# Turning a normalised activation on VectorE in 32x32 blocks, in one layer of a hybrid encoder

## The chip, the core and the metric

The kernel runs on one core of a Trainium2 chip. Its time is the device time of one execution in microseconds. The names of the engines in the profile are PE (TensorE's matmuls), PEld (TensorE's weight loads), DVE (VectorE), ACT (ScalarE), POOL (GpSimd) and SP (SyncE, which here only issues DMAs). Two runs are compared by their medians; a single profiled execution gives the trace.

## The reference

One encoder layer on 2048 tokens of 1024 features, all float32:

```python
h  = rms_norm(x, norm_mix)
z  = h @ w_in                       # 1024 x 4352, split into q, k, v of two attentions and two gates
yA = windowed_gqa(qA, kA, vA, sink) # 8 heads of 64, window 128
yB = neighborhood_attn(qB, kB, vB, rpb)   # 32 x 64 grid, 8 x 16 neighbours
gates  = sigmoid(gate + b_gate)
merged = gateA * (yA @ w_proj_a) + gateB * (yB @ w_proj_b)
x  = x + merged @ w_out
h2 = rms_norm(x, norm_mlp)
x  = x + square(relu(h2 @ w_up)) @ w_down
out = rms_norm(x, norm_final)
```

rms_norm divides each token's row by its root mean square and multiplies each feature by a gain.

## The kernel before

Tokens go in four blocks of 512 (BT). A float32 product is made from three TensorE passes: each operand is split into a rounded high part, a cast on ScalarE, and the rest, a subtraction on VectorE or GpSimd (`split`, L246 to L249), and `mm3s` issues high x high, high x low and low x high (L252 to L254; `mm3` with L201 to L203 likewise). The large projections use a seven-product scheme over quarters (`in_quad`, `up_quad`), whose sums and differences of quarters are made on VectorE and GpSimd.

TensorE contracts over the partitions, so an activation must stand with features on partitions. After normalisation it stands with tokens on partitions, and has to be turned. Before the change TensorE does this against an identity matrix, in tiles of 128x128, and ScalarE evicts the result from PSUM with the feature's gain as the scale, which by then is one number per partition.

The stages, in the order of the profile:

- The in-projection of blocks 0 and 1 (to about 335 us). Both blocks are turned in SBUF (`turned`, `scaled`, `scaled_less`), and seven pages of h, the right operands of the seven products, are built from them. The page for product 5 is the first whose sum runs on GpSimd (the loop over `halves(t1)` after `normalised(xp, tiles[1], by_scalar=True)`). The square roots of a normalisation are also GpSimd operations (`rstd_of`, L229), so on that engine they stand in one row with these sums. While quads q = 5 and 6 run, blocks 2 and 3 of x are normalised, turned by 64 TensorE transposes (L242), evicted into two buffers `ze` (L464) and stored to DRAM in `h1d` (L602).
- Attention A (about 335 to 700) with the in-projection of blocks 2 and 3, whose pages `h_pages` loads from `h1d` and splits; then attention B (to about 1010).
- Four blocks b of gates, merge and out-projection (about 1010 to 1437). `gated` projects y and multiplies by the gate; POOL adds the two branches, `mh` and `ml` (L1265, L1266) are the split sum, the out-projection adds to x (`xr`, L1284), and the result is normalised, turned by 32 TensorE transposes for each block (L1295), evicted with `g_mlp` (L1301) and stored to `h2d` from the ScalarE queue (L174). In block 3 the evictions go into the space of `mh`.
- The up projection (about 1437 to 2077). `up_right` loads blocks of `h2d` and builds the pages `ubh1` to `ubh7` of the seven products; the one for product 2 is loaded into `urb`. `up_quad` takes the products in the order 1, 5, 6, 2, 7, 4, 3 and stores the squared activations. `up_start` prepares the first pages and weights ahead of the last block's out-projection.
- The down projection (about 2077 to 2680), with the final normalisation.

A scheduler orders the instructions of each engine from the program and its pools of buffers; `tc.issue_after(x)` forces an instruction behind another. Each engine works through its own row in order and waits at its head, and so does each DMA queue's issuer (SP, and the ScalarE queue).

Of the kernel before, what the change touches and what calls it, by code (L numbers as in the profile page):

```python
# [22 lines left out]
P = 128  # L23
# [69 lines left out]
def encoder_layer(ctx, tc, x, norm_mix, w_in, b_gate, sink, rpb, w_pa, w_pb, w_out,  # L93
# [39 lines left out]
    g_mlp = cp.tile([P, KC], F32, name="g_mlp")  # L133
# [80 lines left out]
    def load_tile(pl, tag, bufs, rows):  # L214
        t = T(pl, [P, D], F32, tag, bufs)
        last_dma[0] = SY.dma_start(t, rows).ins
        return t

    def rstd_of(pl, t, jp=None, mean=False):

        st = T(pl, [P, 4], F32, "st", 4)
        junk = T(pl if jp is None else jp, [P, 512], F32, "junk", 1)
        for n in range(2):
            A.activation(junk, t[:, n * 512 : (n + 1) * 512], AF.Square, scale=float(D) ** -0.5 if mean else 1.0,
                         accum_out=st[:, n : n + 1])
        r = st[:, 2 : 3]
        V.scalar_tensor_tensor(out=r, in0=st[:, 0:1], scalar=EPS if mean else D * EPS, in1=st[:, 1:2],
                               op0=ALU.add, op1=ALU.add)
        G.tensor_tensor(out=r, in0=r, in1=power, op=ALU.pow)  # L229
        return r  # L230

    def normalised(pl, tiles, jp=None, by_scalar=False):

        for t in tiles:
            if by_scalar:
                A.activation(t, t, AF.Copy, scale=rstd_of(pl, t, jp, True))
            else:
                V.tensor_scalar(t, t, rstd_of(pl, t, jp), float(D) ** 0.5, ALU.mult, ALU.mult)

    def turned(ps, tiles, k):  # L240
        for t in range(4):
# [240 lines left out]
    tiles[1] = x_tiles(xp, 1, 8)  # L482
    ws1.append(row_half(*QUADS[1], 1))
    with tc.issue_after(last_dma[0]), nc.allow_non_contiguous_dma(reason="small per-feature vectors"):
        SY.dma_start(g_mlp, norm_mlp[0].rearrange("(k p) -> p k", p=P))
# [15 lines left out]
    next(quad0)  # L501
    next(quad0)
    normalised(xp, tiles[1], by_scalar=True)
    for o, h, l in zip(halves(t1), *map(halves, right[1])):
        add(G, o, h.bitcast(F32), l.bitcast(F32))
    next(quad1)
    next(quad1)

# [72 lines left out]
    for q in range(2, len(QUADS)):  # L581
        if q == 5:
            s_v.close()
            in_v2.pop()
            xp = pools(s_z, "right", ("xin", "st"), "x2")
        if q == 7:
            bias_tables()
        lf = list(in_left(ws, 256, (1, 2) if q == 2 else ()))
        if q + 1 < len(QUADS):
            ws = in_weights(*QUADS[q + 1])  # L590
        if q in (5, 6):

            b = q - 3
            xt = x_tiles(xp, b, 3)
            normalised(xp, xt, Junk())
            for k in range(0, KC, 2):
                ht = in_e()
# [4 lines left out]
                SY.dma_start(h1d[b - 2][k * P : (k + 2) * P, :].rearrange("(k p) t -> p k t", p=P), ht)  # L602
# [338 lines left out]
    flush(queue=SY)  # L941
    s_b.close()
    s_pg = ExitStack()
    p4 = pools(s_pg, "right", ("page", "yraw", "z"), "m")

    def load_y(b):
        yh, yl = [], []
# [27 lines left out]
    p4x = pools(s_wo, "left", ("xr", "junk", "mh", "ml"), "m")  # L975

    p4x["st"] = cp
    wo = []

    def load_wo(n):  # L980
# [169 lines left out]
        parts(3, b22)  # L1150

    def squared(c, src=None):
        A.activation(c, c if src is None else src, AF.Relu)  # L1153
        A.activation(c, c, AF.Square)

    def up_quad(m, q, lf, right, spread):

        x, y, z = [None] * 2, [None] * 2, [None] * 2
        c1, u2, c11, c22 = [None] * 2, [None] * 2, [None] * 2, [None] * 2

        def keep(n, a, c):
            stored[0] = SY.dma_start(ats[n][2 * q + a][:, m], c).ins

        for n in (1, 5, 6, 2, 7, 4, 3):
            hl, (rh, rl) = lf[n], right[n]
            last = None
            for a in range(2):
# [9 lines left out]
                    mm3s(ps, hl[:, 0, k, at], hl[:, 1, k, at], rh[:, k], rl[:, k], k == 0 and n in (1, 5, 6), k == 3)  # L1177
                if n == 1:
                    c1[a] = up_rings["c"]()
                    A.copy(c1[a], ps)  # L1180
                elif n == 6:
                    u2[a] = up_rings["c"]()
                    last = add(V, u2[a], ps, c1[a])
                elif n == 2:
                    c11[a] = up_rings["c"]()
                    squared(c11[a], ps)
                    keep(1, a, c11[a])
                elif n == 7:
                    c22[a] = up_rings["c"]()
                    add(V, c22[a], ps, c1[a])  # L1190
                    last = add(V, c22[a], z[a], c22[a])
                    squared(c22[a])
                    keep(4, a, c22[a])
                elif n == 4:
                    last = add(V, c1[a], ps, c1[a])
                    squared(c1[a])
                    keep(2, a, c1[a])
                elif n == 3:
                    a11, a12, a21, a22 = c11[a], c1[a], u2[a], c22[a]
                    last = add(V, a21, ps, a21)  # L1200
# [27 lines left out]
    for b in range(NB):  # L1228
# [59 lines left out]
        flush()  # L1288
        if b < NB - 1:
            next_y = load_y(b + 1)  # L1290
        normalised(p4x, tiles)
        for k in range(KC):
            ps = psum("av", 1) if b < NB - 1 or k % 3 == 0 else psum("pt", 2)
            for t in range(4):
                PE.transpose(ps[:, t * P : (t + 1) * P], tiles[t][:, k * P : (k + 1) * P], ident)  # L1295
# [5 lines left out]
            A.activation(ht, ps, AF.Copy, scale=g_mlp[:, k : k + 1])  # L1301
# [215 lines left out]
```

## Time and profile before

| | |
|---|---|
| runs | 2684.27, 2681.82, 2678.03 us; median 2681.82 |
| profiled execution | 2680.99 us, its span 2679.2 us |
| mean granted TensorE clock | 0.998 |
| PE busy | 2613.9 us, 98% of the span |
| DVE / ACT / POOL busy | 1535.4 (57%) / 1260.7 (47%) / 839.1 (31%) |
| DMA | 490.28 MB moved, mean 183 GB/s |

A row of the profile's groups names line, engine, operation, written and read buffers, count, busy time and mean duration in ns, and then the time that its engine sat idle ahead of it, with what released it. A row of the timeline gives start, duration, engine, operation, and in brackets the idle time before it and its releaser. A row of a source line's view gives the shortest, median and longest duration in ns and the first and last start. A row of the waits gives waiting and releasing operation, total us, times, longest.

### The profile page before, as it was taken

The page shows a single profiled execution, that of the slowest core. Times are in us where ns is not written, and L with a number is a line of the kernel's source. Part 1 is how long each engine was busy: PE and PEld are TensorE (multiplying, and loading weights), DVE is VectorE, ACT ScalarE, POOL GpSimd, SP SyncE. Part 2 cuts the span into 40 slices and gives each one's busy share as a digit, 9 for nine tenths or more (in the row PEclk, how much of TensorE's full clock was granted, in tenths as well). Part 3 has the DMA queues.
Part 4 walks back from the last instruction along what each step waited for, and adds up shares of the span by engine and source line. Part 5 has one row for each costly group of instructions (what it writes and reads, how often), then busy time and mean ns, then how long its engine had stood idle before and what let it go on. Part 6 is the DMA issues. An engine that isn't in the chain of part 4 may idle for free. (4 is left out here: it accounts for less than half of the span.)

```text
span 2679.2 us, 34877 instructions
## 1 busy us (share of the span) xinstructions
PE 2613.9 (98%) x12332; PEld 2168.2 (81%) x12332; DVE 1535.4 (57%) x2288; ACT 1260.7 (47%) x2297; POOL 839.1 (31%) x671
## 2 busy tenths in 40 slices
PE   7999999999999999999999999999999999999998
PEld 5788878777888888887777888878888888888887
DVE  7756446665544444533447666775565635555667
ACT  7334346666555555533334544454445232332444
POOL 1211234334555542532231554664562000000011
PEclk9999999999999999999999999999999999999999
DMA  5655384455876755745545665764436935445555
GB/s 181 196 157 189 135 251 129 115 150 154 231 221 185 197 165 183 238 136 178 181 150 188 208 224 202 270 212 157 162 112 234 327 124 173 149 146 169 183 184 176
DMA packets 334079, 490.28 MB, mean 183 GB/s; under 512 B 27321, under 2 KB 162617, under 8 KB 331729
## 3 DMA queue, kind: packets, MB, share of 16 engines
q1 hardware_dynamic: 322384, 462.89, 54.7%
q10 hardware_dynamic: 11520, 25.17, 2.5%
q8 instruction: 97, 1.59, 0.2%
q14 instruction: 78, 0.63, 0.1%
HBM read 328.52 MB, written 159.45 MB: 182 GB/s over the span
## 5 line engine op out<-in xcount | busy, mean ns | idle before, releaser
L253 PE MATMUL b<-dwh,dah 128*128 128x512 f32 x896 | 348.7, 389 | 0.0
L254 PE MATMUL b<-dwh,dah 128*128 128x512 f32 x896 | 347.8, 389 | 0.0
L252 PE MATMUL b<-dwh,dah 128*128 128x512 f32 x896 | 338.1, 389 | 1.0 <-ACT dwh L248 1.0
L245 POOL TENSOR_TENSOR uc<-uc,uc 128x512 f32<-128x512 f32 x120 | 236.3, 1984 | 195.4 <-issue 93.3
L248 ACT CAST dah<-da 128x1024 fp32r<-128x1024 f32 (+1 forms) x128 | 121.0, 945 | 365.0 <-PE b L254 240.9
L249 DVE TENSOR_TENSOR dah<-da,dah 128x1024 fp32r<-128x1024 f32 (+1 forms) x128 | 139.3, 1089 | 217.5 <-ACT dah L248 212.7
L252 PE MATMUL b<-ubh,uwhlb 128*128 128x512 f32 x592 | 230.5, 390 | 3.3 <-DVE uc L245 1.7
L254 PE MATMUL b<-ubh,uwhlb 128*128 128x512 f32 x592 | 229.6, 390 | 1.2 <-DVE uwhlb L249 1.2
L253 PE MATMUL b<-ubh,uwhlb 128*128 128x512 f32 x592 | 230.2, 389 | 0.0
L201 PE MATMUL mm<-hT,whl 128*128 128x512 f32 x544 | 219.2, 403 | 0.0
L203 PE MATMUL mm<-hT,whl 128*128 128x512 f32 x544 | 215.8, 397 | 0.0
L202 PE MATMUL mm<-hT,whl 128*128 128x512 f32 x544 | 215.0, 395 | 0.0
L178 POOL TENSOR_TENSOR whl<-raw,whl 128x1024 fp32r<-128x1024 f32 x66 | 160.2, 2427 | 146.5 <-ACT whl L177 125.9
L1407 POOL TENSOR_TENSOR st<-st,power 128x1 f32<-128x1 f32 x16 | 13.6, 858 | 613.4 <-DVE st L1406 613.3
L252 PEld LDWEIGHTS b<-dwh,dah 128*128 128x128 f32 x896 | 168.1, 188 | 36.3 <-ACT dwh L248 1.4
L253 PEld LDWEIGHTS b<-dwh,dah 128*128 128x128 f32 x896 | 168.2, 188 | 35.4 <-DVE dwh L249 0.4
L254 PEld LDWEIGHTS b<-dwh,dah 128*128 128x128 f32 x896 | 168.2, 188 | 34.7
L252 PE MATMUL zb<-zh,zwhl 128*128 128x512 f32 x476 | 186.7, 394 | 5.9 <-DVE zc L245 1.6
L254 PE MATMUL zb<-zh,zwhl 128*128 128x512 f32 x476 | 183.6, 392 | 4.6 <-DVE zwhl L249 4.5
L245 DVE TENSOR_TENSOR uc<-b,uc 128x512 f32<-128x512 f32 x160 | 108.5, 687 | 137.3 <-PE b L254 128.7
L253 PE MATMUL zb<-zh,zwhl 128*128 128x512 f32 x476 | 186.0, 391 | 0.0
L252 PEld LDWEIGHTS b<-ubh,uwhlb 128*128 128x128 f32 x592 | 111.1, 188 | 26.8 <-issue 2.1
(252 smaller groups left out, 6183.1 us busy)
## 6 DMA issues: line engine op xcount, KB each, us to landing
at<-uc SPq DMA_DIRECT2D x224, 256.0 KB
da<-at SPq DMA_DIRECT2D x96, 512.0 KB
dw<-in_w_down_dram SPq DMA_DIRECT2D x160, 256.0 KB
uraw<-in_w_up_dram SPq DMA_DIRECT2D x32, 1024.0 KB
raw<-in_w_in_dram SPq DMA_DIRECT2D x34, 512.0 KB
zraw<-in_w_in_dram SPq DMA_DIRECT2D x16, 1024.0 KB
z<-zg SPq DMA_DIRECT2D x64, 256.0 KB
qa<-qs_a SPq DMA_DIRECT2D x32, 256.0 KB
```

The lines of the kernel that those rows point to most:

```text
L178: G.tensor_tensor(out=hl[:, 1], in0=raw, in1=hl[:, 0].bitcast(F32), op=ALU.subtract)
L201: PE.matmul(ps, lh, rh, start=first, stop=False)
L202: PE.matmul(ps, lh, rl, start=False, stop=False)
L203: PE.matmul(ps, ll, rh, start=False, stop=last)
L245: return eng.tensor_tensor(out=out, in0=a, in1=b, op=op).ins
L248: A.copy(hi, src)
L249: return eng.tensor_tensor(out=lo, in0=src, in1=hi.bitcast(F32), op=ALU.subtract).ins
L252: PE.matmul(ps, lh, rh, start=first, stop=False, skip_group_check=True)
L253: PE.matmul(ps, lh, rl, start=False, stop=False, skip_group_check=True)
L254: PE.matmul(ps, ll, rh, start=False, stop=last, skip_group_check=True)
L1407: G.tensor_tensor(out=r, in0=r, in1=power, op=ALU.pow)
```

## The change

Blocks 2 and 3 of h and all four blocks of h2 are no longer turned by TensorE. `turned_out` handles a block in four groups of 256 features: four VectorE transpositions (one for each tile of 128 tokens), which turn each 32x32 square where it stands, one VectorE multiplication of 128x1024 by the gain, and four stores on SP. Each store takes 32 partitions and puts the squares at their place in DRAM in pieces of 128 floats. The gain has now to be laid out as squares are, so `turned_gain` loads the vector as four squares and turns it on VectorE; `g_mlp`, its load and the ScalarE evictions go. In DRAM the tokens within a block of 512 stand in another order (a t c in place of t a c); the readers undo it by views: `h_pages` in its splits, `up_quad` when it reads PSUM. The squares' unused output of h2's normalisation goes to a PSUM bank (`Unused`). Three buffers `ht` take the stores of blocks 0 to 2; block 3 still uses the space of `mh`. Last, the two GpSimd sums of the first page are forced behind the third and fourth root of block 1.

```diff
+    roots = []
...
-        G.tensor_tensor(out=r, in0=r, in1=power, op=ALU.pow)
+        roots.append(G.tensor_tensor(out=r, in0=r, in1=power, op=ALU.pow).ins)
...
+    def turned_out(d, ht, tiles, g, gain=None, queue=None):
+        hv = ht.rearrange("p (j t c) -> p t j c", j=8, t=4)
+        for t in range(4):
+            V.transpose(out=hv[:, t], in_=tiles[t][:, g * 256 : (g + 1) * 256].rearrange("p (j c) -> p j c", j=8))
+        h3 = ht.rearrange("p (j x) -> p j x", j=8)
+        if gain is not None:
+            (step, n), _ = gain.ap
+            gv = bass.AP(gain.tensor, gain.offset + 8 * g, [[step, n], [1, 8], [0, P]])
+            V.tensor_tensor(out=h3, in0=h3, in1=gv, op=ALU.mult)
+        dv = d.rearrange("(j i) (a x) -> a i j x", i=32, a=4)
+        for a in range(4):
+            (queue or SY).dma_start(dv[a][:, 8 * g : 8 * g + 8], h3[32 * a : 32 * a + 32])
+
+    def turned_gain(t, norm):
+        for a in range(4):
+            SY.dma_start(t[32 * a : 32 * a + 32, 32:64], norm[0].rearrange("(j i) -> j i", i=32))
+        V.transpose(out=t[:, 0:32], in_=t[:, 32:64])
+        return t[:, 0:32]
+
+    def by_token(c):
+        return c.rearrange("p (t a c) -> p t a c", t=4, a=4)
+
+    def by_place(c):
+        return c.rearrange("p (a t c) -> p t a c", t=4, a=4)
...
-        SY.dma_start(g_mlp, norm_mlp[0].rearrange("(k p) -> p k", p=P))
...
-    for o, h, l in zip(halves(t1), *map(halves, right[1])):
-        add(G, o, h.bitcast(F32), l.bitcast(F32))
+    for n, (o, h, l) in enumerate(zip(halves(t1), *map(halves, right[1]))):
+        with tc.issue_after(roots[6 + n]):
+            add(G, o, h.bitcast(F32), l.bitcast(F32))
...
+            xp = pools(s_z, "right", ("xin", "st", "gt"), "x2")
+            gain = turned_gain(T(xp, [P, 64], F32, "gt", 1), norm_mix)
...
-            for k in range(0, KC, 2):
-                ht = in_e()
-                for i in range(2):
-                    ps = zbank(tpool, 2)
-                    turned(ps, xt, k + i)
-                    scaled(ht[:, i], ps, k + i)
-                SY.dma_start(h1d[b - 2][k * P : (k + 2) * P, :].rearrange("(k p) t -> p k t", p=P), ht)
+            for g in range(4):
+                turned_out(h1d[b - 2], in_e().rearrange("p k x -> p (k x)"), xt, g, gain)
...
-                split(raw, hh, ll, V)
+                for k in range(2):
+                    split(by_place(raw[:, k]), by_token(hh[:, k]), by_token(ll[:, k]), V)
...
+    gain = turned_gain(T(p4x, [P, BT], F32, "gt", 1)[:, 0:64], norm_mlp)
+    class Unused:
+        def tile(self, *a, **k):
+            return psum("av", 1)
...
+        def plus(out, ps, c):
+            return add(V, by_token(out), by_place(ps), by_token(c))
...
-                    A.copy(c1[a], ps)
+                    A.copy(by_token(c1[a]), by_place(ps))
...
-        normalised(p4x, tiles)
-        for k in range(KC):
-            ps = psum("av", 1) if b < NB - 1 or k % 3 == 0 else psum("pt", 2)
-            for t in range(4):
-                PE.transpose(ps[:, t * P : (t + 1) * P], tiles[t][:, k * P : (k + 1) * P], ident)
+        normalised(p4x, tiles, Unused())
+        for g in range(4):
             if b == NB - 1:
-                h2 = T(p4x, [P, KC, BT], F32R, "mh", 1).bitcast(F32) if k == 0 else h2
-                ht = h2[:, k]
+                h2 = T(p4x, [P, KC, BT], F32R, "mh", 1).bitcast(F32) if g == 0 else h2
+                ht = h2[:, 2 * g : 2 * g + 2].rearrange("p k x -> p (k x)")
             else:
-                ht = T(p4, [P, BT], F32, "yraw", 6)
-            A.activation(ht, ps, AF.Copy, scale=g_mlp[:, k : k + 1])
-            put(h2d[b][k * P : (k + 1) * P, :], ht)
-            flush(1)
-    flush()
+                ht = T(p4, [P, 2 * BT], F32, "ht", 3)
+            turned_out(h2d[b], ht, tiles, g, gain)
```

More of the change, by code (lines that the diff above doesn't have):

```diff
@@ L132, in encoder_layer @@
     g_mix = cp.tile([P, KC], F32, name="g_mix")
-    g_mlp = cp.tile([P, KC], F32, name="g_mlp")
     bg = cp.tile([P, 16], F32, name="bg")
@@ L584, in encoder_layer @@
             in_v2.pop()
-            xp = pools(s_z, "right", ("xin", "st"), "x2")
+            xp = pools(s_z, "right", ("xin", "st", "gt"), "x2")
+            gain = turned_gain(T(xp, [P, 64], F32, "gt", 1), norm_mix)
         if q == 7:
@@ L943, in encoder_layer @@
     s_pg = ExitStack()
-    p4 = pools(s_pg, "right", ("page", "yraw", "z"), "m")
+    p4 = pools(s_pg, "right", ("page", "yraw", "z", "ht"), "m")
     def load_y(b):
@@ L974, in encoder_layer @@
     pwo = pool("pwo", side="left", stack=s_wo)
-    p4x = pools(s_wo, "left", ("xr", "junk", "mh", "ml"), "m")
+    p4x = pools(s_wo, "left", ("xr", "gt", "mh", "ml"), "m")
     p4x["st"] = cp
+    gain = turned_gain(T(p4x, [P, BT], F32, "gt", 1)[:, 0:64], norm_mlp)
+    class Unused:
+        def tile(self, *a, **k):
+            return psum("av", 1)
     wo = []
@@ L1152, in squared @@
     def squared(c, src=None):
-        A.activation(c, c if src is None else src, AF.Relu)
+        if src is None:
+            A.activation(c, c, AF.Relu)
+        else:
+            A.activation(by_token(c), by_place(src), AF.Relu)
         A.activation(c, c, AF.Square)
@@ L1179, in up_quad @@
                     c1[a] = up_rings["c"]()
-                    A.copy(c1[a], ps)
+                    A.copy(by_token(c1[a]), by_place(ps))
                 elif n == 6:
                     u2[a] = up_rings["c"]()
-                    last = add(V, u2[a], ps, c1[a])
+                    last = plus(u2[a], ps, c1[a])
                 elif n == 2:
@@ L1189, in up_quad @@
                     c22[a] = up_rings["c"]()
-                    add(V, c22[a], ps, c1[a])
-                    last = add(V, c22[a], z[a], c22[a])
+                    plus(c22[a], ps, c1[a])
+                    last = plus(c22[a], z[a], c22[a])
                     squared(c22[a])
@@ L1194, in up_quad @@
                 elif n == 4:
-                    last = add(V, c1[a], ps, c1[a])
+                    last = plus(c1[a], ps, c1[a])
                     squared(c1[a])
@@ L1199, in up_quad @@
                     a11, a12, a21, a22 = c11[a], c1[a], u2[a], c22[a]
-                    last = add(V, a21, ps, a21)
+                    last = plus(a21, ps, a21)
                     squared(a21)
```

## The prediction

> **What bounds the kernel now.** I read the page first (span, busy shares, slices), then windows of the two stages that lose transposes, then the groups by line, and then the waits and the timeline wherever the new order of instructions differs.
>
> ```profile
> span 2679.2 us, 34877 instructions
> PE 2613.9 (98%) x12332; PEld 2168.2 (81%) x12332; DVE 1535.4 (57%) x2288; ACT 1260.7 (47%) x2297; POOL 839.1 (31%) x671
> PE   7999999999999999999999999999999999999998
> PEclk9999999999999999999999999999999999999999
> ```
>
> TensorE is the bound: 2613.9 of 2679.2 us busy, 65 us idle in all. An instruction taken from it shortens the kernel unless something else is late; an engine at 57% matters only where TensorE waits for it. The windows below give PE, PEld, DVE, ACT and POOL busy time, granted clock, DMA share and GB/s. The third is the second half of h alone, transposes only.
>
> ```profile
> 225.00:300.00 75.00, 73.79 (x355) 60.52 (x354) 41.91 (x51) 36.26 (x65) 17.85 (x16) 1.00 0.58 200
> 1160.00:1435.00 275.00, 268.34 (x1216) 217.83 (x1215) 128.94 (x150) 107.58 (x176) 82.91 (x54) 1.00 0.51 169
> 225.00:300.00 75.00, 9.08 (x64) 7.76 (x64) 0.00 (x0) 1.00 0.58 200
> ```
>
> The 64 transposes lie in a stage that TensorE fills (73.79 of 75). VectorE is idle 75 − 41.91 = 33.1 us there, and 275 − 128.94 = 146 us in the three gate-and-merge blocks.
>
> **The change part by part.** *Transposes removed: 64 for h, 96 for blocks 0 to 2 of h2, 32 for block 3.* Their busy time includes a latency that the next matmul overlaps, so I price them by starts in the timeline:
>
> ```profile
> 1441.92 0.39 PE L252 MATMUL b<-ubh,uwhlb 128*128 128x512 f32 x1
> 1442.15 0.40 PE L253 MATMUL b<-ubh,uwhlb 128*128 128x512 f32 x1
> 1442.38 0.49 PE L1295 MATMUL pt<-ident,xr 128*128 128x128 f32 x3
> 1442.63 0.47 PE L254 MATMUL b<-ubh,uwhlb 128*128 128x512 f32 x1
> 1442.95 0.40 PE L252 MATMUL b<-ubh,uwhlb 128*128 128x512 f32 x1
> PE av L1295 <- ACT yraw L1301: 2.1, 3, 1.5
> ```
>
> A matmul follows the last after 0.2265 us (0.23 as rounded). From 1442.38 to 1442.95 pass 0.57 us for one matmul and three transposes: (0.57 − 0.2265)/3 = 0.1145 each. So h gives 64 × 0.1145 = −7.3 and h2 96 × 0.1145 = −11.0. The last row is a wait of TensorE for the evictions of these transposes between 1160 and 1435: −2.1. Block 3 is counted at the hand-over.
>
> *VectorE's new work.* Neither operation is in the trace. Nearest rows:
>
> ```profile
> L249 DVE TENSOR_TENSOR dwh<-dt,dwh 128x512 fp32r<-128x512 f32 x64 | 43.8, 684 | 0.0
> L1266 DVE TENSOR_TENSOR ml<-z,mh 128x512 fp32r<-128x512 f32 x32 | 55.3, 1729 | 70.9 <-ACT mh L1265 70.9
> 25.97 0.16 DVE L227 SCALAR_TENSOR_TENSOR st<-st 128x1 f32<-128x1 f32 x1 [2.45 <-ACT junk L224]
> 28.57 1.22 DVE L249 TENSOR_TENSOR zwhl<-zraw,zwhl 128x1024 fp32r<-128x1024 f32 x1
> ```
>
> One column takes 0.16 us, 512 take 0.684: about 1 ns a column, so a transposition of 256 columns is 0.16 + 0.26 = 0.42 us. Its bounds are 0.16 and 0.69; I take 0.42, since the price grows evenly with columns (1024 cost 1.22). The gain multiplication over 1024 columns costs 1.22, up to 2.5 times that if it meets POOL as L1266 does (1729 against 684). A block then takes 16 × 0.42 + 4 × 1.22 = 11.6 us of VectorE: two blocks of h 23.2 of the 33.1 idle, three of h2 35 of 146. The idle time covers it, but every group queues in order behind VectorE's other work.
>
> The Trainium skill, "VectorE: DVE Perf Modes", section "Rules for kernel authors", says to turn 128x128 on TensorE where a PSUM destination will do, and has VectorE turn 32x32 blocks only, which speaks against this change. By that rule nothing would be gained; the trace instead shows TensorE full and VectorE not, and the stores place the blocks.
>
> *Stores.* Before, h1d takes 8 issues on SP and h2d 32 on ACT; after, SP issues 16 per block, of 512-byte pieces like those of y_a:
>
> ```profile
> L174 SPq DMA_DIRECT2D y_a<-ya x32: 574/586/1480, 404.5 to 679.9; - x32
> L174 ACTq DMA_DIRECT2D h2d<-yraw x24: 326/327/373, 1170.0 to 1393.8; - x24
> L602 SPq DMA_DIRECT2D h1d<-ze x8: 360/370/727, 237.2 to 290.0; - x8
> ```
>
> Between 0.33 and 0.586 each (min/median/max in ns), I take 0.575 for its pieces are alike: 9.2 us of SP a block. In h they hold the next weight loads, and a third group's transposition waits for a landed store of its buffer (there are two), with VectorE's additions that free TensorE's banks queued behind it: +2, between 0 and 5. In the gate stage 12 of a block's 16 stores stand ahead of gate loads and the last projection weights on SP: +4, between 0 and 10. These are choices within bounds: some 5 to 10 us of SP's row, of which prefetching should hide more than half.
>
> *First page's sums behind the second block's roots.*
>
> ```profile
> 16.23 4.75 POOL L245 TENSOR_TENSOR zraw<-zh,zh 128x1024 f32<-128x1024 f32 x2 [4.59 <-DVE zh L467]
> 18.70 3.36 DVE L249 TENSOR_TENSOR zwhl<-zraw,zwhl 128x1024 fp32r<-128x1024 f32 x1
> 22.12 0.50 PE L254 MATMUL zb<-zh,zwhl 128*128 128x512 f32 x1 [2.48 <-DVE zwhl L249]
> ```
>
> Beside POOL's sums a VectorE split took 3.36 instead of 1.22, and TensorE waited 2.48 for it. With the sums later, 3.36 − 1.22 = −2.1 (between −2.5 and 0: the later sums run from about 27.7, beside the split at 28.57, which may then be the slow one). That is also how this part may not do what it says.
>
> *Edits costed at nothing.*
>
> ```profile
> L485 SPq DMA_DIRECT2D g_mlp<-in_norm_mlp_dram x1: 545/545/545, 11.3 to 11.3; - x1
> L390 DVE SCALAR_TENSOR_TENSOR z<-mm,z x10: 678/684/692, 383.1 to 503.1; 128x512 fp32r<-128x512 f32 x10
> L386 DVE TENSOR_TENSOR z<-mm,z x16: 673/886/1137, 521.7 to 746.4; 128x512 fp32r<-128x512 f32 x16
> ```
>
> The gains' four small loads replace one of 0.545 issued at 11.3, so they are out by 13.5, and VectorE's turn of the gain that waits for them stands after 26; if they came late, the weight splits queued behind it would be late by as much. Reading in another order shows no price: L386 reads PSUM rearranged and can take 673 as L390's plain read does. The squares' unused output goes to a PSUM bank that the transposes leave free. ScalarE's lost evictions are worth nothing beyond the 2.1.
>
> *First attention unit.* In the new order of instructions 24 projection matmuls and 6 score matmuls stand between its first scores and its first transposition of probabilities. Before, there was nothing:
>
> ```profile
> 384.09 0.34 PE L704 MATMUL s<-ka,qa 128*128 128x384 f32 x1
> 387.89 0.69 PE L722 MATMUL pt<-ident,sa 128*128 128x128 f32 x2 [3.46 <-POOL sa L716]
> 389.65 0.63 PE L201 MATMUL mm<-hT,whl 128*128 128x512 f32 x1
> 390.08 0.63 PE L202 MATMUL mm<-hT,whl 128*128 128x512 f32 x1
> 385.00:402.00 17.00, 14.11 (x63) 12.05 (x64) 7.32 (x26) 8.51 (x26) 9.26 (x15) 0.80 0.85 254
> ```
>
> A stall of 3.46 us, then a granted clock that averages 0.80 over the window: 12 matmuls start 0.427 apart instead of 0.2265, 2.4 more. So 5.9 can go. 24 × 0.2265 plus six scores is 6.5 us of cover; but the same softmax work then runs beside them, and some stall may move: −4, between −5.9 and 0.
>
> *Hand-over to the up stage.* TensorE does known work until it needs the second product's page (ubh2), whose space is the one from which block 3 of h2 is stored, so its cast waits for all 16 stores.
>
> ```profile
> 1436.93 0.39 PE L203 MATMUL pt<-wo,ml 128*128 128x512 f32 x1
> 1437.36 0.69 DVE L1284 TENSOR_TENSOR xr<-pt,xr 128x512 f32<-128x512 f32 x1 [2.33 <-PE pt L203]
> L245 DVE TENSOR_TENSOR uc<-b,uc 128x512 f32<-128x512 f32 x160 | 108.5, 687 | 137.3 <-PE b L254 128.7 <-POOL uwhlb L249 2.6 <-POOL uc L245 1.8
> 1438.44 4.63 DVE L249 TENSOR_TENSOR ubh<-uraw,ubh 128x1024 fp32r<-128x1024 f32 x4 [0.39 <-ACT ubh L248]
> 1443.81 0.75 DVE L238 TENSOR_SCALAR xr<-xr,st 128x1024 f32<-128x1024 f32 x1 [0.66 <-POOL st L229]
> 1453.69 0.33 ACTq L174 DMA_DIRECT2D h2d<-mh  x1
> 1458.58 1.04 ACT L248 CAST ubh<-urb 128x1024 fp32r<-128x1024 f32 x1 [0.91 <-DMA h2d<-mh]
> 1459.68 0.50 PE L252 MATMUL b<-ubh,uwhla 128*128 128x512 f32 x1 [3.09 <-ACT ubh L248]
> ```
>
> Let T0 = 1437.16, one pitch after the last output matmul's start. Before, 22.52 us pass to 1459.68 for 74 matmuls (74 × 0.2265 = 16.76): 5.76 lost to 32 transposes and stalls. After, TensorE's order holds 87 matmuls there, 19.7 us. VectorE's order is: last residual addition (done at T0 + 0.9), 8 transposes 3.36, four page splits 4.63, weight split, 0.15, split, sum (1.22 each), normalisation 0.75, two additions 0.69 each, 4 transposes 1.68, first gain 1.22: T0 + 17.7. SP then issues 16 × 0.575: T0 + 26.9. From the last store's issue end (1453.69 + 0.33) to the cast (1458.58) pass 4.5 us, 0.91 of it idle; I take 3.3 of landing, between 2 and 4.5. The cast, 1.05: T0 + 31.3. Stall 31.3 − 19.7 = 11.6, plus 2.4 of slow clock as after the stall at 387.89: 14.0, net 14.0 − 5.76 = **+8.2**. Low end: issues of 0.33 (all issued by T0 + 23), landing 2: stall 6.3, no slow clock, net +0.5. High end: transposes of 0.69 and landing 4.5: +12.6.
>
> The Trainium skill, "TensorE: Matmul & The Clock Gate", section "What's actually happening", gives a halved clock after about 3.4 us idle. The row at 387.89 agrees (3.46, then 0.427 apart); without that rule the 2.4 stands on the row.
>
> *Sum against the profiled run* (2680.99 us, its span 2679.2 and 1.8 around it; 0.83 below the median 2681.82): −7.3 − 11.0 − 2.1 − 2.1 − 4 + 8.2 + 2 + 4 = −12.3, so 2668.7, as a median **2669.5**. All good ends: −7.3 − 11.0 − 2.1 − 2.5 − 5.9 + 0.5 = −28.3, 2653.5. All bad ends (removed evictions' wait and sums worth nothing): −18.3 + 12.6 + 5 + 10 = +9.3, 2691.
>
> **The rivals.** *Covers hold everywhere.* Stores issue in 0.33 and loads stay ahead: −7.3 − 11.0 − 2.1 − 2.1 − 5.9 + 0.5 + 3 = −24.9, 2656.9. For it speaks the idle VectorE, against it the 586 ns rows. Chance 0.18.
>
> *Gains given back.* The attention stall only moves, SP's row of stores costs +8 and +3: −22.5 + 8 + 3 + 8.2 = −3.3, 2678.5. Within 0.2% of before (5.4 us, about what a measurement here can tell from no change). For it speaks the two-buffer wait. Chance 0.14.
>
> *Slower: VectorE's block operations run f times as long.* In h they then need 23.2 f of 33.1 idle us, and at the hand-over the first store moves by (f − 1) × (12 × 0.42 + 1.22) = 6.3 (f − 1). At f = 1.75 that is 7.5 + 4.7, and the forecast gain is gone; from f = 1.9 it is slower by over 0.2%. At f = 2.5, as L1266 beside POOL (1729 against 684), 24.9 + 9.4 + 3 × (3.05 − 2.3) for gains now slower than SP's four issues = 36.6: 2706. Against it: POOL is busy only 17.85 of the 75 us in h. Chance 0.16.
>
> The Trainium skill, "VectorE: DVE Perf Modes", section "The three transpose paths", has 311 ns for a bf16 128x128 as 32x32 blocks on VectorE; nothing here shows it.
>
> **How the numbers follow.** Forecast 0.52, the rivals 0.18, 0.14 and 0.16. Faster = 0.52 + 0.18 = 0.70, same 0.14, slower 0.16. The range, 2655 to 2690, reaches from just above the good ends' sum to the bad ends' sum; what it leaves out is most of the slow VectorE (0.14) and the luckiest part of the covers (0.04).
>
> **What would show it.** Right: no L242 work on h1d's blocks nor L1295's on TensorE; VectorE transposes near 0.42 and multiplications near 1.22; SP issues near 0.575; TensorE's wait at 22 under 0.5; no 3.5 us stall at the first attention unit; one stall near 11 before the first ubh2 matmul with a clock below 1.00 behind it; TensorE's idle time up by some 2 in h and 4 in the gate stage. Wrong: transposes above 0.75, TensorE waiting for VectorE through 225 to 300, or over 20 us lost at the hand-over.

## The result and the profile after

The changed kernel takes 2699.86 us (median of 6 runs, 2697.34 to 2702.35) against 2680.82 before (6 runs): ratio 1.0073, 95% interval 1.0060 to 1.0086. It is slower by some 19 us, where 12 us faster was forecast, and lies outside the range. The head of its page:

```profile
span 2697.3 us, 34681 instructions
PE 2620.9 (97%) x12140; PEld 2159.8 (80%) x12140; DVE 1600.8 (59%) x2418; ACT 1230.6 (46%) x2257; POOL 850.4 (32%) x671
```

TensorE has 192 instructions fewer (12140 against 12332) and yet is busy 7 us longer (2620.9 against 2613.9), and idle 76 us instead of 65. So two things went wrong: the instructions that are left take longer, and new waits came.

One reason for the longer instructions is the granted clock, the share of full speed that TensorE is given. These are the profiled executions of the kernel before and of the changed kernel, and then three windows of the changed kernel (PE, PEld, DVE, ACT and POOL busy, granted clock, DMA share, GB/s) in which the kernel before has a clock of 1.00:

```profile
core 0: 2679.2 us, clock 0.998
core 0: 2697.3 us, clock 0.992
32.00:41.00 9.00, 8.57 (x33) 6.84 (x34) 3.60 (x6) 5.23 (x8) 3.74 (x2) 0.81 0.24 60
251.00:262.00 11.00, 7.10 (x21) 4.69 (x20) 10.55 (x13) 1.28 (x2) 0.00 (x0) 0.71 0.97 313
1475.00:1485.00 10.00, 9.87 (x31) 7.47 (x32) 9.93 (x9) 7.28 (x10) 0.06 (x1) 0.70 0.30 96
```

Each of the three windows lies at or behind a new wait. All six runs of the changed kernel have a mean clock of 0.992 or 0.993, and 18 later runs of the kernel before 0.995 to 0.998, 0.9967 on average. As an estimate from these means, (1 − 0.9925) × 2699.9 = 20 us against (1 − 0.9967) × 2681.6 = 9 us: some 11 us more are lost to a lower clock. The saved transposes, the new waits themselves and what follows stand beside this term.

To see where, I took from the two timelines the start of the same matmul, counted among its kind, and formed the difference:

| matmul | before, at us | changed kernel later by |
|---|---|---|
| in-projection, 72nd | 39.9 | 3.1 |
| in-projection, 356th | 112.0 | 3.6 |
| in-projection, 853rd (ahead of h's second half) | 229.8 | 5.6 |
| in-projection, 1350th | 350.7 | 8.4 |
| first with a page of hT | 371.0 | 9.4 |
| 82nd with hT | 410.6 | 11.6 |
| last with hT | 1058.1 | 18.0 |
| last of the out-projection (T0 of the prediction) | 1436.9 | 7.7 |
| up stage, 671st | 1595.0 | 15.8 |
| down stage, 2601st | 2651.0 | 17.6 |

The two terms that the prediction worked out most closely look right: the gate stage, whose first matmuls start at 1058, gained 10.3 (forecast 11.0 + 2.1 − 4 = 9.1), and the hand-over gave back 8.1 (forecast 8.2). Both numbers hold matmuls of the up stage that only changed places. The rows count the matmuls that read ubh, ahead of T0 and then from T0 to the first one with ubh2, first in the kernel before and then in the changed kernel:

```profile
1400.00:1437.16 37.16, 6.45 (x26) 4.80 (x26) 4.79 (x4) 4.11 (x4) 0.00 (x0) 1.00 0.54 190
1437.16:1459.67 22.51, 14.28 (x58) 10.59 (x58) 6.99 (x6) 6.97 (x8) 0.00 (x0) 1.00 0.74 248
1400.00:1444.84 44.84, 3.14 (x13) 2.63 (x14) 4.71 (x4) 4.11 (x4) 0.00 (x0) 1.00 0.47 167
1444.84:1475.08 30.24, 20.45 (x87) 15.98 (x86) 4.60 (x5) 4.99 (x6) 0.00 (x0) 0.93 0.57 170
```

Thirteen of them, 13 × 0.2265 = 2.9 us, moved behind T0. Without them the gate stage gained 7.4 and the hand-over gave back 5.2. Everything ahead of 1058 was forecast as −7.3 − 2.1 − 4 + 2 = −11.4 and is +18.

A large part of that has no wait at all. From 112 to 230 us and from 411 to 1058 the changed kernel falls behind steadily. These rows of its timeline stand on the two sides of the place where that ends; ten matmuls lie between the first two and ten between the last two:

```profile
1073.76 0.40 PE L201 MATMUL mm<-hT,whl 128*128 128x512 f32 x1
1076.10 0.40 PE L202 MATMUL mm<-hT,whl 128*128 128x512 f32 x1
1076.33 0.40 PE L200 MATMUL mm<-page,whl 128*128 128x512 f32 x1
1078.61 0.39 PE L201 MATMUL mm<-page,whl 128*128 128x512 f32 x1
```

With the moving page hT a matmul takes (1076.10 − 1073.76)/10 = 0.234 us, with the next page 0.228, at the same granted clock and with the same weights' buffer. Averaged over the trace, 128x512 matmuls start 0.2333 apart for the pages zh1, zh2, zh4, zh6 and zh7 (0.2271 to 0.2277 before), 0.2285 and 0.2288 for zh3 and zh5, 0.2329 for hT (0.2288 before), and 0.2266 to 0.2270 in the up and down stages, as before. The program says what these pages have in common: g_mlp was a tile of 32 bytes a partition, and with it gone every buffer behind it on the left side lies 32 bytes lower. zh1 starts at byte 1952 instead of 1984, so no longer at a multiple of 64. The pages zh3, zh5, page and ubh, both operands of the down stage (dwh and dah) and the weights zwhl, whl, uwhla and uwhlb lie on the right side and did not move.

VectorE's and SP's new work, by source line (shortest, median and longest in ns):

```profile
L249 DVE STREAM_TRANSPOSE ht<-xr x48: 393/403/447, 1147.3 to 1377.4; 128x256 f32<-128x256 f32 x48
L254 DVE TENSOR_TENSOR ht<-ht,gt x12: 1179/1756/3420, 1183.6 to 1378.9; 128x1024 f32<-128x1024 f32 x12
L257 SPq DMA_DIRECT2D h2d<-ht x48: 303/464/1404, 1184.9 to 1383.7; - x48
```

A transposition takes 0.40 (forecast 0.42), a multiplication 1.18 where POOL is idle and up to 3.4 beside it, a store's issue 0.46 (forecast 0.575). The hand-over in the timeline:

```profile
1444.61 0.40 PE L202 MATMUL pt<-wo,ml 128*128 128x512 f32 x1
1460.55 5.91 DVE L254 TENSOR_TENSOR mh<-mh,gt 128x1024 f32<-128x1024 f32 x4
1463.08 8.50 SPq L257 DMA_DIRECT2D h2d<-mh  x16
1473.99 1.99 ACT L282 CAST ubh<-urb 128x1024 fp32r<-128x1024 f32 x2 [8.38 <-DMA h2d<-mh]
1475.09 1.22 PE L286 MATMUL b<-ubh,uwhla 128*128 128x512 f32 x2 [8.22 <-ACT ubh L282]
```

T0 is 1444.61 + 0.23 = 1444.84. The first store is issued at T0 + 18.2 (forecast 17.7), the last is out at T0 + 26.7 (26.9), the cast starts at T0 + 29.2 (30.2) and TensorE goes on at T0 + 30.3 (31.3). Its stall is 8.22 rather than 11.6, for part of the time was already lost ahead of it. That chain held link by link; what it was compared with did not, as the part on the prediction's steps says.

### The profile page after: what moved, and what is told of

The parts are those of the page before. It is cut to its first block, busy times and chain, and to the rows that moved or that the text cites. A ratio compares the mean times of both kernels' runs of the same rounds, so it can differ in the third digit from the quotient of the medians.

```text
span 2697.3 us, 34681 instructions
## 1 busy us (share of the span) xinstructions
PE 2620.9 (97%) x12140; PEld 2159.8 (80%) x12140; DVE 1600.8 (59%) x2418; ACT 1230.6 (46%) x2257; POOL 850.4 (32%) x671
## 3 DMA queue, kind: packets, MB, share of 16 engines
q8 instruction: 96, 1.57, 0.2%
## 5 line engine op out<-in xcount | busy, mean ns | idle before, releaser
L177 POOL TENSOR_TENSOR whl<-raw,whl 128x1024 fp32r<-128x1024 f32 x66 | 165.6, 2510 | 158.8 <-ACT whl L176 140.4
L286 PE MATMUL zb<-zh,zwhl 128*128 128x512 f32 x476 | 190.8, 402 | 12.1 <-DVE zc L279 6.3
L287 PE MATMUL zb<-zh,zwhl 128*128 128x512 f32 x476 | 190.0, 399 | 0.0
L288 PE MATMUL zb<-zh,zwhl 128*128 128x512 f32 x476 | 187.3, 399 | 1.8 <-DVE zwhl L283 1.8
```

Of the source, the lines that this page charges most:

```text
L177: G.tensor_tensor(out=hl[:, 1], in0=raw, in1=hl[:, 0].bitcast(F32), op=ALU.subtract)
L286: PE.matmul(ps, lh, rh, start=first, stop=False, skip_group_check=True)
L287: PE.matmul(ps, lh, rl, start=False, stop=False, skip_group_check=True)
L288: PE.matmul(ps, ll, rh, start=False, stop=last, skip_group_check=True)
```

## The experiments

**The 32 bytes.** Four kernels moved buffers and nothing else: the changed kernel with the room kept, and the kernel before with the left side, both sides, or the right side moved.

```diff
 e1_room (changed kernel):
     g_mix = cp.tile([P, KC], F32, name="g_mix")
+    room = cp.tile([P, KC], F32, name="room")
...
+    G.memset(room, 0.0)
 e2_left_shift (kernel before):
-    warm = cp.tile([P, 1], F32, name="warm")
+    warm = bg[:, 0:1]
 e3_both_shift (kernel before):
-    g_mlp = cp.tile([P, KC], F32, name="g_mlp")
+    g_mlp = cr.tile([P, KC], F32, name="g_mlp")
 e4_right_shift (kernel before): e2's and e3's edits together
```

> The changed kernel with 32 unused bytes a partition kept where g_mlp lay, so that every buffer allocated behind it stands where it stood before (the pages zh1 at byte 1984 instead of 1952). Nothing else differs. Theory 'address': in the changed kernel matmuls whose moving page was shifted by 32 bytes start 0.2333 us apart instead of 0.2267 (zh1, zh2, zh4, zh6, zh7: 1020 matmuls; hT 1632, there 0.0041 on average), so 1020 x 0.006 + 1632 x 0.0041 = 12.8 us and some for the attention's own matmuls come back: 2699.9 - 13 to 16 = 2684 to 2687, with a pace of 0.2267 all the way. Rival 'engine': the slower pace comes from VectorE's block transpositions or their gain's layout, from 27 us on: pace stays 0.233 until about 1076, time 2700. Either way about 4 to 9 us are left in the start, the stage of h and the hand-over.

> The kernel before, with its one-element warm-up tile laid into another tile, so that the buffers of the left side alone shift down by 32 bytes (zh1 at 1952, hT at 1952), as in the changed kernel; weights on the right stay. Theory 'address': pace 0.2333 for zh1, zh2, zh4, zh6, zh7 and hT, 0.2267 for zh3, zh5, page, ubh; 13 to 16 us slower than before, 2694 to 2697. Rival 'engine': no change, 2681 and 0.2267 throughout.

> The kernel before, with g_mlp moved to the right side, so that both sides shift by 32 bytes: moving pages and weights all stand at 32 beyond a multiple of 64. Theory 'moving': a moving page off a multiple of 64 bytes costs 0.0066 us a matmul whatever the weights do: some 9100 matmuls of 512 columns x 0.0066 = 60, 2741 us, pace 0.2333 in the up and down stages too. Theory 'pair': only a moving page that stands otherwise within 64 bytes than its weights is slow (in the changed kernel wo and mh are both shifted and run at 0.2275): pace 0.2267 everywhere, 2681. Theory 'engine': 2681.

> The kernel before, left side shifted by 64 bytes and right side by 32: pages zh1, hT, wo stand at a multiple of 64, weights zwhl, whl, uwhl, dwh and pages zh3, zh5, page, ubh, dah 32 beyond it. Theory 'moving': fast for zh1 and hT (0.2267), slow (0.2333) for zh3, zh5, page, ubh, dah: 408 + 768 + 2688 + 2688 matmuls x 0.0066 = 43, 2724. Theory 'pair': slow for zh1, zh2, zh4, zh6, zh7 and hT, fast for the rest: as with the left shift alone, 2694 to 2697. Theory 'engine': 2681.

e1_room: 2687.55 us (8 runs), ratio to before 1.0025 (1.0014 to 1.0035), against 1.0073 with the shift. e2_left_shift: 2688.22 (10 runs), 1.0027 (1.0017 to 1.0036): the kernel before, with nothing of the change in it, becomes slower by 7 us through the place of its buffers. e3_both_shift: 2678.10 in one run, within the spread of before. e4_right_shift: 2689.93 in one run, above all 18 runs of before. Rows of three timelines, ten matmuls apart in each pair: e2_left_shift, e3_both_shift and e4_right_shift in the in-projection (page on the left, weights on the right), then e4_right_shift in the up stage (both on the right):

```profile
150.13 0.40 PE L253 MATMUL zb<-zh,zwhl 128*128 128x512 f32 x1
152.46 0.40 PE L254 MATMUL zb<-zh,zwhl 128*128 128x512 f32 x1
```

```profile
150.13 0.39 PE L252 MATMUL zb<-zh,zwhl 128*128 128x512 f32 x1
152.39 0.39 PE L253 MATMUL zb<-zh,zwhl 128*128 128x512 f32 x1
```

```profile
150.18 0.40 PE L253 MATMUL zb<-zh,zwhl 128*128 128x512 f32 x1
152.51 0.40 PE L254 MATMUL zb<-zh,zwhl 128*128 128x512 f32 x1
...
1901.23 0.39 PE L254 MATMUL b<-ubh,uwhla 128*128 128x512 f32 x1
1903.49 0.39 PE L252 MATMUL b<-ubh,uwhla 128*128 128x512 f32 x1
```

The distances are 0.233, 0.226, 0.233 and 0.226. The theory "moving" falls, since with both at 32 the pace is the fast one, and so does "engine", since no VectorE transposition is in these kernels. "Pair" stands: slow is the matmul whose moving page and weights start 32 bytes apart within 64. Averaged over the trace, hT takes 0.2329 with the left side moved, 0.2330 with the right, 0.2290 with both. The out-projection of the changed kernel fits too: wo and mh both moved, and its pace is 0.2260 to 0.2285. What the chip does there is not shown. Nor is it shown that 64 is the number that counts: in the addresses of the built programs every one of these fast pairs starts a multiple of 512 bytes apart and every slow one 32 bytes short of that, and no other distance was tried.

The size came out at half of what was expected, for the expectation of 13 to 16 us added up all slow matmuls. The trace of e2_left_shift is 7.2 us late at 1058 and 4.3 at the end.

The Trainium skill, "SBUF — State Buffer", section "Operand start alignment", lets an operand start at any multiple of its element size and adds that this is about legality, not speed. The kernels here run with such starts, as the page has it, and the runs put a price on the second half: 0.0066 us on a matmul of 0.2267.

The room has a second effect: the scheduler orders the hand-over otherwise (20 up matmuls come earlier), for a reason that is not shown. In e1_room's trace it gives back 3.6 instead of 8.1. So of the 12 us between the changed kernel and e1_room some 8 are left for the pace, an estimate by subtraction.

**The parts, one at a time,** with all addresses as before:

```diff
 e6_roots: kernel before + roots, issue_after(roots[6 + n]) on the first page's two sums
 e7_h: kernel before + turned_out, turned_gain, by_place in h_pages, for blocks 2 and 3 of h
 e8_h2: kernel before + the same for h2, and
-    g_mix = cp.tile([P, KC], F32, name="g_mix")
+    g_mix = cp.tile([P, 2 * KC], F32, name="g_mix")[:, 0:KC]
 e9_h2_three: as e8_h2, but in block 3
+            turned(ps, tiles, k)
+            A.activation(by_place(ht), by_token(ps), AF.Copy, scale=g_mlp[:, k : k + 1])
```

> The kernel before with one part of the change alone: the first page's two GpSimd sums behind the third and fourth root of block 1. All addresses stay. Forecast of the prediction: -2.1, 2679.5. Theory 'roots': with the addresses restored the whole change is 1.4 us late at the 72nd in-projection matmul and 3.9 at the 356th (a wait of 2.37 for VectorE's ze at 30.7 and one of 1.91 at 102.4), because the later sums slow VectorE's splits of the next products: +2 to +4, 2684 to 2686, with the same waits in its trace. Rival 'loads': the four small loads of the gain on SP made that: then -2 to 0, 2680 to 2682, and no such waits.

> The kernel before with the second half of h alone turned on VectorE (and its four small gain loads), all addresses as before. Prediction: -7.3 + 2 for new waits and -4 for the first attention unit = -9, 2672. Theory 'h row': VectorE's transpositions wait for landed stores of the two ze buffers, with the zc additions that free TensorE's banks queued behind (waits of 1.19, 2.92 and 0.95 at 252 to 286, then half clock): the 64 transposes saved are given back and the first attention unit waits for qa's load instead of for its softmax: 0 to +5, 2681 to 2687. Rival 'no row': the loss in the whole change came from the late start only, and h alone gains 5 to 9: 2672 to 2677.

> The kernel before with h2 alone turned on VectorE, all addresses as before (32 unused bytes in g_mlp's place). Prediction: -11.0 - 2.1 + 4 + 8.2 = -0.9. Theory 'row read': the whole change with addresses restored gained 13.5 between 1058 and 1437 and gave 3.4 back at the hand-over and 1.4 to 2.7 later: -6 to -9, 2673 to 2676. Rival: the gate stage's gain there was a catching up after the late start: -1 to +3, 2681 to 2685.

> As with h2 alone, but only blocks 0 to 2; block 3 is turned by TensorE as before, its ScalarE evictions writing the tokens in the stored order. All addresses as before. If the hand-over's 16 stores behind VectorE's queue are what is given back there, the stage keeps its gain of 9 to 13 and the hand-over is as before (5.8 lost): 2669 to 2673. If the gain in the gate stage is only made by the late start: 2680 to 2683.

| | us | ratio to before (95%) |
|---|---|---|
| e6_roots | 2683.02 | 1.0001 (0.9991 to 1.0010) |
| e7_h | 2690.78 | 1.0029 (1.0017 to 1.0040) |
| e8_h2 | 2674.02 | 0.9968 (0.9955 to 0.9980) |
| e9_h2_three | 2674.87 | 0.9975 (0.9964 to 0.9986) |

h2 is the good part and h the bad one. The roots make no difference that the runs can tell; their trace is 1.7 us late at the 72nd matmul:

```profile
26.14 3.09 POOL L247 TENSOR_TENSOR zraw<-zh,zh 128x1024 f32<-128x1024 f32 x1
27.05 3.26 DVE L251 TENSOR_TENSOR zwhl<-zraw,zwhl 128x1024 fp32r<-128x1024 f32 x1
30.24 0.68 DVE L392 SCALAR_TENSOR_TENSOR ze<-zb,ze 128x512 fp32r<-128x512 f32 x1
30.97 0.50 PE L254 MATMUL zb<-zh,zwhl 128*128 128x512 f32 x1 [1.97 <-DVE ze L392]
```

The sum now runs beside the next split, which takes 3.26 instead of 1.22, and TensorE waits 1.97 behind it instead of 2.48 at the first. By the starts of its matmuls it was 2.2 us ahead at 23 us and level at 31. The rest of the 1.7 us is clock, granted at 0.81 behind that wait where the kernel before has 1.00:

```profile
32.00:41.00 9.00, 8.98 (x36) 7.02 (x35) 3.45 (x6) 6.53 (x11) 2.87 (x2) 0.81 0.24 60
```

e8_h2 gained 10.8 between its gate stage's start and the end of the out-projection and gave 5.1 back later; in both numbers 2.9 us are again the 13 up matmuls that stand behind T0. At the hand-over it waits for a weight split that stands behind the gains on VectorE:

```profile
1444.35 8.57 SPq L255 DMA_DIRECT2D h2d<-mh  x16
1451.48 0.80 PE L286 MATMUL b<-ubh,uwhlb 128*128 128x512 f32 x1 [3.28 <-DVE uwhlb L281]
```

Leaving block 3 to TensorE (e9_h2_three) is no better, nor is spreading its stores over two queues:

```diff
 e13_h2_two_queues (e8_h2, block 3 only):
-            (queue or SY).dma_start(dv[a][:, 8 * g : 8 * g + 8], h3[32 * a : 32 * a + 32])
+            (SY, A)[a // 2].dma_start(dv[a][:, 8 * g : 8 * g + 8], h3[32 * a : 32 * a + 32])
```

> h2 alone on VectorE, addresses as before, and of block 3's 16 stores at the hand-over eight go on the ScalarE queue and eight on SP. SP's 16 issues took 8.57 us and the cast that waits for them came 2.3 us behind the last. Theory 'issue': the last store is issued some 2.5 to 4 us earlier, the stall before the second product shrinks by as much and with it the half clock: 2670 to 2673 against 2674. Rival: the gains on VectorE (5.87 us) set the last store anyway, or another weight split is waited for there (3.28 for uwhlb): no change.

2674.28 us (10 runs), ratio 0.9981 (0.9972 to 0.9991). The rival stands: the issue of the stores is no longer what is waited for in this order.

**Why h loses.** By the starts of the same matmuls e7_h stands to the kernel before at −1.7 us once the first transposes are saved (249 us), +3.5 at 267, +1.1 at 302, +4.2 at 369, +6.5 at 411, +7.3 at 1058. Four kernels tested the first of these losses, and a fifth runs both halves of the change together:

```diff
 e10_h_bank (e7_h):
-            normalised(xp, xt, Junk())
+            normalised(xp, xt, Bank())      # tile() gives zbank(tpool, 2)
 e11_h_actq (e7_h):
-                turned_out(h1d[b - 2], in_e().rearrange("p k x -> p (k x)"), xt, g, gain)
+                turned_out(h1d[b - 2], in_e().rearrange("p k x -> p (k x)"), xt, g, gain, A)
 e12_all_mended: h as in e10_h_bank and e11_h_actq, h2 as in e8_h2
 e14_h_no_gain (e10_h_bank): turned_out(..., xt, g)
 e15_h_twice (e10_h_bank):
-        for t in range(4):
+        for t in (0, 0, 1, 1, 2, 2, 3, 3):
             V.transpose(out=hv[:, t], ...)
```

> The kernel with h alone turned on VectorE (2690.8, 0.29% slower than before), and the squares' unused output of h's normalisation in a PSUM bank instead of the two ze buffers, so that eight ScalarE uses of these two buffers go. Theory 'two buffers': ScalarE waited 9.8 us in two places for stores of ze to land before it could write its squares' output there, and the chain from these squares to the transposition to zc's additions is what TensorE waited for (2.64 at 251.8): these waits go or halve, -3 to -6 against h alone, 2685 to 2688. Rival 'row': VectorE's own queue (transpositions and gains, 11.6 us a block) delays zc whoever writes the squares: no change, 2689 to 2692.

> The kernel with h alone turned on VectorE, and h's 32 stores issued from the ScalarE queue instead of SP. Theory 'SP row': SP's 32 issues of 0.47 us hold the next loads, among them those of the first attention units (qa's load is waited for 4.53 us at 405): -3 to -7, 2684 to 2688. Rival 'landing': the stores land no earlier and the waits for the ze buffers stay; ScalarE, blocked for 15 us more, is late with its casts: 0 to +3, 2690 to 2694.

> Both halves of the change (h and h2 on VectorE), addresses as before, without the moved roots, with both mends of h: squares' output in a PSUM bank and h's stores on the ScalarE queue. If the two mends make h worth its 64 transposes (-7): 2666 to 2669. If h stays a loss of 5 to 9: 2679 to 2683; the h2 part alone had 2674.

> h alone on VectorE with the squares' output in a PSUM bank (2690.8), and without the eight multiplications by the gain (left out, so the second half of h lacks its gain): VectorE has 9.7 us less to do in that stage, everything else stays. Theory 'row': between 230 and 268 VectorE was busy 34.7 of 38 us (in the kernel before some 22 of the same stretch), so TensorE's waits of 0.5 to 1.5 us for zc and zwhl there are waits for VectorE's own row: they shrink and the stage of h gains 3 to 6, 2685 to 2688. Rival 'stores': the waits are for the landing of stores and the later wait of 2.96 at 360 and the loads of the first attention units make the rest: no change, 2689 to 2692.

> h alone on VectorE with the squares' output in a PSUM bank (2690.8), and each of h's 32 transpositions made twice (32 x 0.41 = 13 us more for VectorE). Theory 'row': TensorE waits for most of what is added, as VectorE has no room left in the two bursts: +7 to +14, 2698 to 2705, all of it between 230 and 300. Rival 'stores': VectorE was idle for the landings and the additions fit into it: 0 to +3, 2691 to 2694.

| | us | ratio to before (95%) |
|---|---|---|
| e10_h_bank | 2690.77 | 1.0039 (1.0024 to 1.0054) |
| e11_h_actq | 2695.41 | 1.0055 (1.0040 to 1.0070) |
| e12_all_mended | 2690.68 | 1.0038 (1.0025 to 1.0051) |
| e14_h_no_gain | 2686.56 | 1.0022 (1.0011 to 1.0033) |
| e15_h_twice | 2698.64 | 1.0069 (1.0052 to 1.0086) |

The first loss lies between 249 and 256 us. Two windows of e7_h (columns as in the windows above):

```profile
235.00:250.00 15.00, 13.01 (x56) 9.91 (x54) 13.62 (x25) 3.14 (x3) 0.00 (x0) 1.00 0.91 255
250.00:268.00 18.00, 16.16 (x59) 12.74 (x60) 12.27 (x18) 9.17 (x22) 1.94 (x3) 0.81 0.56 197
```

VectorE is busy 13.62 of 15 us, then TensorE waits 2.64 us at 251.84 for zc, one of VectorE's additions, and behind that it has a clock of 0.81. Windows of the stretch from 230 to 268 in the kernel before, e10_h_bank, e14_h_no_gain and e15_h_twice, in this order (PE, PEld, DVE, ACT and POOL busy, granted clock, DMA share, GB/s):

```profile
230.00:268.00 38.00, 37.61 (x180) 30.58 (x180) 23.04 (x29) 17.96 (x34) 6.07 (x7) 1.00 0.55 194
```

```profile
230.00:268.00 38.00, 34.66 (x139) 26.38 (x140) 34.67 (x57) 12.74 (x25) 7.71 (x7) 0.96 0.64 195
```

```profile
230.00:268.00 38.00, 36.36 (x156) 29.14 (x157) 30.01 (x52) 13.77 (x27) 8.79 (x8) 1.00 0.66 197
```

```profile
230.00:268.00 38.00, 28.43 (x103) 21.28 (x104) 34.08 (x64) 11.24 (x23) 7.72 (x7) 0.89 0.61 187
```

In e10_h_bank VectorE is busy 34.67 of 38 us where it was 23.04. TensorE waits there 0.52 and 1.46 us for zc, behind VectorE's row, and 1.19 for a cast of zwhl on ScalarE, and the clock falls to 0.96. Adding 13 us of work to VectorE cost 7.9 (forecast of "row" 7 to 14, of "stores" at most 3), and the trace has all of it between 230 and 302. So "row" stands for this stretch and "stores" falls. Taking 9.7 us of work away won 4.2 us (forecast 3 to 6), which is weaker evidence: the intervals of the two ratios overlap, and the trace is 3.8 us ahead of e10_h_bank's at 267 but only 0.8 at 302, because a wait of 2.57 for zc came at 273. Freeing the buffers from the squares' output (e10_h_bank) made no measurable difference in time, though its trace was some 1.3 us better at 302, so "two buffers" falls as far as the squares go. VectorE's transpositions still wait for stores of these two buffers to land (0.28 and 0.71 us at 242 and 245), and no run gave them a third.

The ScalarE queue made it worse, which neither theory had as large. Rows of e11_h_actq:

```profile
250.09 8.06 ACTq L256 DMA_DIRECT2D h1d<-ze  x8
258.24 1.04 ACT L281 CAST zwhl<-zS 128x1024 fp32r<-128x1024 f32 x1 [12.75 <-DMA h1d<-ze]
259.34 0.79 PE L285 MATMUL zb<-zh,zwhl 128*128 128x512 f32 x1 [12.27 <-ACT zwhl L281]
```

A store that waits for VectorE's multiplication (until 250.05) waits at the head of ScalarE's own row, eight stores then take until 258.15, and the weights' cast behind them starts at 258.24 where it started at 247.36 in e7_h. e12_all_mended, which holds this queue too, landed outside both of its forecasts, 17 us above h2 alone.

The losses behind the stage of h are two. h_pages now splits halves of 128x512 with zc's additions queued behind them, and TensorE waits 2.96 us there at 362 (1.57 before). Two such halves take VectorE 4.94 us in e7_h where one split of 128x1024 took 1.91 before, both beside splits on GpSimd:

```profile
356.33 4.94 DVE L282 TENSOR_TENSOR hT<-raw,hT 128x512 fp32r<-128x512 f32 x2 [1.99 <-ACT hT L281]
356.83 1.91 DVE L249 TENSOR_TENSOR hT<-raw,hT 128x1024 fp32r<-128x1024 f32 x1 [3.62 <-ACT hT L248]
```

And the first attention unit's stall only changed its name. The first row is that wait in e7_h's timeline, the second one of its windows:

```profile
404.96 0.66 PE L733 MATMUL s<-ka,qa 128*128 128x384 f32 x1 [4.53 <-DMA qa<-qs_a]
```

```profile
370.00:405.00 35.00, 30.17 (x148) 24.92 (x146) 21.00 (x63) 15.58 (x49) 14.64 (x23) 0.99 0.98 283
```

The wait for the softmax is gone, and 4.53 us for qa's load stand in its place: the DMA engines are 0.98 busy over these 35 us (0.96 in the kernel before). Whether that load was issued late or landed slowly is not shown.

## Why the prediction was wrong, step by step

- **The small edits, costed at nothing, were the step that failed first.** The text weighed g_mlp's load and evictions and not the 32 bytes of its tile. The pace behind it costs 7 us in the kernel before (e2_left_shift) and by the estimate above some 8 in the changed kernel. Nothing in the trace of before could show it, since all its pages are aligned; the addresses of the two built programs would have.
- **New waits were priced by their length alone.** The sum has a slow clock only behind the stalls of the first attention unit and the hand-over. The runs show it behind short waits too (0.81 behind 1.97 us in e6_roots and behind 2.64 us in e7_h), some 11 us in all by the estimate above.
- **First page's sums: −2.1.** In the trace +1.7, in time nothing (0.9991 to 1.0010). The bound named the reason, the split at 28.57 that becomes the slow one in its turn; the value taken was the other end.
- **h: −7.3 and +2.** Measured for the part alone: about +1 to the end of that stage, +8 in all. The transposes' price held (the trace is 1.7 us ahead at 249). The cover failed: 33 us of idle VectorE were summed over 75 us, but the work comes in two bursts, and in the first VectorE has 1.4 of 15 us left in e7_h and 3 of 38 in e10_h_bank. The slower rival had the right engine and the wrong condition: it asked for block operations 1.9 times as long, and the transpositions were as forecast (0.40).
- **First attention unit: −4.** e7_h went from +1.1 to +7.3 between 351 and 1058. The stall moved to a load, as the text feared ("some stall may move"), and the later split added its own.
- **Gate stage: −11.0 − 2.1 + 4.** Nearly right: −10.3 in the changed kernel, −7.4 without the 13 matmuls that moved, for −9.1. Here VectorE has room (128.94 of 275 us busy before).
- **Hand-over: +8.2.** The chain after the change was right, that the number came out (+8.1) was luck. The prediction counted 74 matmuls in the 22.52 us before, and the row above has 58, so not 5.76 but 22.52 − 58 × 0.2265 = 9.4 were lost before, and its own working gives 14.0 − 9.4 = +4.6. Without the 13 matmuls that moved, which it did not have, +5.2 is measured; with them the number comes near 8.2.
- **Sum.** The gate stage, which has room, came out near its forecast; the two stages without (start, h) came out with the other sign, and the pace and the clock were missing. What stays open: the parts alone make +7.8 (h) − 8.6 (h2) + 0.3 = −0.5 us, and e1_room, the whole with the addresses restored, is +6.7 (2.7 either way; some 3 for each of the parts). About 2 us of this gap can be seen. e1_room and e12_all_mended, which hold h and h2 together, wait 1.9 us at 100 to 102 us and then have a clock of 0.87 over 99 to 112, where e6_roots, e7_h and e8_h2 have 1.00. The rest stays open: e1_room's profiled run was the fastest of its eight (2682.96 against a median of 2687.55), so its trace does not show where the others lose.

The best version is h2's part alone with the room kept, 2674.0 us: 0.9968 of before, and 26 us below the changed kernel.

## What to carry to other kernels

Removing or adding a small tile moves every buffer allocated behind it: compare the addresses of the matmuls' operands before and after an edit, and keep a moving operand and its weights from starting 32 bytes apart within 64, the one difference that was tried. Price a new wait of TensorE with the slower clock that can follow it. Cover is counted over the burst in which the work is due, not over the stage: idle time of an engine summed over 75 us says nothing on the 20 us in which it gets two blocks' work. Moving work off a full engine paid here where the receiving engine's queue had nothing that the full engine waited for.

## What the runs showed of the hardware that was not expected

A 128x512 matmul takes 0.2333 us instead of 0.2267 (3% more) when its moving operand and its weights start 32 bytes apart within 64, whichever of the two is at the multiple of 64; with both 32 bytes off it takes 0.2267. The profile has no wait and no lower clock for it: it shows only in the distance of the starts. The length of a wait of TensorE does not tell whether a slower clock follows: 3.34 us at the first attention unit were followed by 1.00 over 385 to 402 us in e2_left_shift, 3.46 by 0.80 in the kernel before, and 1.97 at 31 us by 0.81 in e6_roots. A VectorE 32x32-block transposition of 128x256 float32 takes 0.40 us, and at most 0.45 also where GpSimd is busy all the while; a multiplication of 128x1024 takes between 1.18 alone and 3.4 beside GpSimd.
